# A two-layer gated mixer block on one core: low weight parts by adding DMAs, and a start with unsplit modulation products and six early chunks

## The chip, the core and the metric

The kernel runs on one core of a Trainium2 chip. The core has a matrix engine (PE, with its weight loads shown apart as PEld), three elementwise engines (DVE, ACT, POOL), a queue engine (SP) that issues DMAs, and 16 DMA engines. The metric is the device time of one execution in microseconds. Of three runs of the kernel before, the median is 1831.37 us (1830.43 to 1831.96).

## The reference, cut to what matters

Two layers (DEPTH = 2) work on a sequence `x` of 512 tokens and a context of 256 tokens, both 1024 wide. In each layer a modulation is computed from one vector per stream, the normalized input is scaled and shifted by it, and one wide projection feeds four branches (retention, short convolution, long convolution, attention), which are gated, merged and projected back:

```python
m = silu(c) @ w_mod + b_mod                    # shift, scale, gate: 3 x 1024, for c and for c_ctx
h = rmsnorm(x, norm_w) * (1 + scale) + shift
p = h @ w_in                                   # 6912 columns for the branches, 4 x 1024 for the gates
merged = sum(sigmoid(g_i) * (branch_i @ w_branch[i]) for i in range(4))
x = x + gate * (merged @ w_out)
```

In the second layer the context needs only its keys, values and retention states. All is float32.

## The kernel before, in words

Features lie on the 128 partitions and tokens along the free dimension, so a chunk of 128 output features is a chain of products over eight 128x128 blocks of the weights, accumulated in one PSUM bank. To get float32 accuracy out of the fast `float32r` form, both operands are split into a high part (a rounded copy) and a low part (the value minus its high part); a block then takes three products, high by high, high by low and low by high (`mm3`, L478). A chunk has 24 products: 256 columns each for a context stream, 512 for an `x` stream. There are four streams in a row, named by layer: c0 (context), x0, c1 (context, keys and values only), x1.

Weights are loaded by SP in the order of use (`w_load`, L425): for a context stream as two halves of 128x512 in arena rows, for an `x` stream as one 128x1024 tile in one of two `wraw` buffers. `w_split` (L445) makes the parts in one of three `wt` buffers: ACT copies the high part, DVE subtracts it from the raw tile for the low part. `w_ahead` (L461) keeps two chunks split ahead of the one in use. A gate chunk (kind "g") brings along a 128x512 tile of `w_branch`, split in the same way into arena rows.

The order on PE is written by the program: `Tally` (L191) counts an estimated clock, and `slot` (L337) lets generators of side work (attention, retention, convolutions) put in their products when the estimate says that their inputs are ready and that DVE and ACT aren't too far behind. The other engines' instructions are ordered by the framework, and each engine takes its own in order.

`start` (L1346) is the first stage. The modulation of layer 0 is needed in eight parts b = 0 to 7 before the context's normalized input exists. For each part four tiles of 128x512 of `w_m` are loaded (`mod_load`, L542); `mod_pe` (L559) splits each on ACT and DVE and multiplies with the vectors' four columns (high and low of both streams, `s4`), 16 products of 256 columns into four PSUM partitions; `mod_pe_end` (L572) copies the result to SBUF and turns it onto the partitions with two small products against `sel`. `modulate` (L659) then makes block b of the input, high and low. Beside this the first three projection chunks (ak, av, ax) are multiplied block by block, three iterations behind the modulation (LAG = 3).

Of the kernel before, what the change touches and what calls it, by code (L numbers as in the profile page):

```python
# [22 lines left out]
LAG = 3  # L23
PINS = 3

P = 128
# [164 lines left out]
class Tally:  # L191
# [14 lines left out]
    def add(self, eng, op, a, k):  # L206
# [4 lines left out]
        if eng == "tensor":  # L211
            if op == "transpose":
                d = 0.109
            elif aps[2].dtype == F32:
                d = max(0.218, aps[2].free_size() / 600)
            else:
                d = aps[2].free_size() / 2400
                if aps[2].dtype == F32R and d < 0.1:
                    d = 0.213
            self.now += d  # L220
            end = self.now + 0.15
        else:
# [12 lines left out]
            end = start + d + 0.15  # L235
            if eng == "sync":
                end += 2.0 + n * out.shape[0] / 90000
# [40 lines left out]
class Block:  # L278
    def __init__(self, ctx, tc, xc, vec, cst, w_a, w_g, w_b, w_o, w_m, out, out2):
# [5 lines left out]
        rp = ctx.enter_context(tc.tile_pool(name="rp", bufs=1))  # L285
        rp.tile([P, PAD], F32, name="fill")
        self.arena = Arena(rp, NROWS, 12)
# [9 lines left out]
        self.vec = cp.tile([P, NV], F32, name="vec")  # L297
        nc.sync.dma_start(self.vec, vec)
# [6 lines left out]
        self.turn = {}  # L305
        self.wq, self.wraws, self.wready, self.wkeep = [], [], {}, {}
        self.lanes = [[] for _ in range(5)]
        self.turns = 0
# [73 lines left out]
    def get_banks(self, n):  # L382

        while True:
            i = self.turn.get("work", 0)
            ready = max(self.nc.over(self.work[(i + j) % 4]) for j in range(n))
# [38 lines left out]
    def w_load(self):  # L425
# [4 lines left out]
        if small:  # L430
            raws = [(self.row(), slice(o, o + 512)) for o in (0, 512)]
            for r, o in raws:
                nc.sync.dma_start(r.a, src[:, o])
            raws = [(r, r.a, o) for r, o in raws]
        else:
            raw = self.take("wraw")
            nc.sync.dma_start(raw, src)
            raws = [(None, raw, slice(0, 1024))]
        if kind == "g":
            r = self.row()  # L440
            nc.sync.dma_start(r.a, self.wsrc["b"][l, i])
            raws.append((r, r.a, None))
        self.wraws.append((key, raws))

    def w_split(self):  # L445
        nc = self.nc
        key, raws = self.wraws.pop(0)
        parts = [self.take("wt")]
        for _, raw, o in raws:
            if o is None:  # L450
# [77 lines left out]
    def csilu(self):  # L528
# [8 lines left out]
        nc.vector.tensor_scalar(self.cs.rearrange("p a b -> p (a b)"), t2, 0.5, None, op0=ALU.mult)  # L537
        self.s4 = self.cp.tile([P, KC, 4], F32R, name="s4")
        nc.scalar.activation(self.s4[:, :, 0:2], self.cs, AF.Copy)
        nc.vector.tensor_tensor(self.s4[:, :, 2:4], self.cs, self.s4[:, :, 0:2].bitcast(F32), op=ALU.subtract)  # L540

# [16 lines left out]

    def mod_pe(self, tiles):  # L559
        nc = self.nc  # L560
        ps = self.bank_now()
        for h, t in enumerate(tiles):
            hi, lo = self.part(), self.part()
            nc.scalar.activation(hi.r, t.a, AF.Copy)
            nc.vector.tensor_tensor(lo.r, t.a, hi.a, op=ALU.subtract)
            for i, x in enumerate((hi, lo)):
                for k in range(2):
                    nc.tensor.matmul(ps[0:4, 0:256], self.s4[:, 2 * h + k], x.r[:, k * 256:k * 256 + 256],
                                     start=(h == 0 and i == 0 and k == 0), stop=(h == 3 and i == 1 and k == 1))
        return ps  # L570

    def mod_pe_end(self, l, b, ps):  # L572
        m4 = self.small("m4", [4, 256], 4)
        self.nc.scalar.activation(m4, ps[0:4, 0:256], AF.Copy)
        for j in range(2):
            self.nc.tensor.matmul(ps[:, 256 + 2 * j:258 + 2 * j], m4[:, cs(j)], self.c("sel")[0:4],
                                  start=True, stop=True)
        self.mod_add(l, b, ps[:, 256:], 2)
# [759 lines left out]

    def load_row(self, st, k):

        o, w = (0, SEQ) if st.s == 0 else (SEQ, CTX)
        x = self.row(w)
        self.nc.sync.dma_start(x.a, self.xd[st.s][k] if st.l else self.xc[k, :, o:o + w])
        return x

    def start(self, st):  # L1346

        nc = self.nc
        loads = [self.mod_load(0, 0)]
        st.x = self.load_x(st)  # L1350
        self.csilu()
        acc = None
        for k in range(KC):
            acc = self.square(st.x[k].a, acc)
        names = [("ak", 0), ("av", 0), ("ax", 0)]
        self.early = {}
        ws, pss = [], []
        mods = {}

        def dense(k):  # L1360
            for w, ps in zip(ws, pss):
                self.mm3(ps, w, [None] * k + [st.hx[k]] + [None] * (KC - 1 - k), ks=[k])

        for k in range(KC + LAG):
            if k + 1 < KC:
                loads.append(self.mod_load(0, k + 1))
            if k < 3:
                ws.append(self.w_get("a", st, CIDX[names[k]], False)[0])
                pss.append(self.take("dense")[:, :st.t])
                self.early[st, CIDX[names[k]]] = pss[-1]  # L1370
            if k < KC:
                mods[k] = self.mod_pe(loads.pop(0))
            if 1 <= k <= KC:
                self.mod_pe_end(0, k - 1, mods.pop(k - 1))
            if k == 1:
                res = []
                for _ in self.rms(acc, res):
                    pass
# [6 lines left out]
        st.x = st.rstd = None  # L1385

# [123 lines left out]
```

## Time and profile before

| what | value |
|---|---|
| median of three runs | 1831.37 us |
| profiled execution, its own time | 1828.66 us |
| its span from first to last instruction | 1826.9 us |
| mean granted clock of PE | 0.997 |
| matrix products | 10242 |
| DMA traffic | 232.60 MB, mean 127 GB/s |

The span is the time between the first and the last instruction of the profiled execution; its own time has 1.8 us around it. The trace gives for each instruction its engine, its start and its length, what ended the idle time before it, and for each DMA the time from issue to landing. Products overlap in their pipeline, so the time that one more product costs is the distance between starts, not its length. Nearly all instructions stand under line 187, the helper that records them, so groups go by tile names: `w`, `wh` and `wl` are a raw weight tile and its parts, `r` an arena row, `d` a PSUM bank of the chunks, `k` a working bank, `s` the modulation's vectors, `s_m` the copied modulation, `cst` constants.

### The profile page before, as it was taken

What the parts mean: (1) busy time and instruction counts of PE and PEld (TensorE: products, weight loads), DVE (VectorE), ACT (ScalarE), POOL (GpSimd) and SP (SyncE); (2) the same over time, 40 slices, a digit from 0 to 9 for tenths busy, and PEclk for the clock granted to TensorE, in tenths of its full rate; (3) what the DMA queues carried; (4) which work ended last, traced back from release to release, by engine and by line L of the source; (5) the groups of instructions that cost most, each with busy time, mean ns of one, the idle gap of its engine ahead of it and who ended that gap; (6) DMA issues with size and microseconds to landing.
All of it is one profiled execution on the core that took longest, in us unless ns stands there. A gap on an engine that the chain in (4) does not pass through costs nothing. (4 is left out here: it accounts for less than half of the span.)

```text
span 1826.9 us, 27582 instructions
## 1 busy us (share of the span) xinstructions
PE 1798.4 (98%) x10242; PEld 1562.3 (86%) x10242; DVE 1326.9 (73%) x2635; ACT 851.6 (47%) x1625; POOL 27.9 (2%) x34
## 2 busy tenths in 40 slices
PE   6999999999999999999999999999999999999998
PEld 4999999988888888888888889888888888888888
DVE  8899999884556669996998457447999866344445
ACT  6666765553554544423423246445534554323223
POOL 1000000000000000000000000000000000000000
PEclk9999999999999999999999999999999999999999
DMA  9646477743222222233555552322222232332233
GB/s 315 246 129 207 120 239 231 233 138 116 70 70 68 83 81 80 95 113 124 183 167 170 159 190 76 116 70 70 65 92 84 84 95 91 111 105 90 87 116 116
DMA packets 104135, 232.60 MB, mean 127 GB/s; under 512 B 12864, under 2 KB 19776, under 8 KB 104000
## 3 DMA queue, kind: packets, MB, share of 16 engines
q1 hardware_dynamic: 104000, 230.84, 39.1%
q8 instruction: 80, 1.31, 0.3%
q14 instruction: 55, 0.45, 0.1%
HBM read 218.73 MB, written 5.24 MB: 123 GB/s over the span
## 5 line engine op out<-in xcount | busy, mean ns | idle before, releaser
L187 PE MATMUL d<-r,wh 128*128 128x512 f32 (+1 forms) x3136 | 942.8, 383 | 0.3 <-DVE r L187 0.3
L187 PEld LDWEIGHTS d<-r,wh 128*128 128x128 f32 x3136 | 572.7, 188 | 106.2 <-DVE r L187 0.8
L187 PE MATMUL d<-r,wl 128*128 128x512 f32 (+1 forms) x1568 | 597.6, 381 | 0.0
L187 DVE TENSOR_TENSOR wl<-w,wh 128x1024 fp32r<-128x1024 f32 x193 | 235.8, 1222 | 234.7 <-ACT wh L187 228.8
L187 ACT ACTIVATE wh<-w 128x1024 fp32r<-128x1024 f32 x193 | 204.9, 1062 | 412.0 <-PE d L187 354.8
L187 PEld LDWEIGHTS d<-r,wl 128*128 128x128 f32 x1568 | 294.8, 188 | 57.8
L187 ACT ACTIVATE r<-r 128x512 fp32r<-128x512 f32 (+3 forms) x264 | 150.6, 588 | 206.6 <-DVE r L187 93.8
L187 DVE TENSOR_TENSOR r<-r,r 128x512 fp32r<-128x512 f32 (+5 forms) x337 | 207.6, 630 | 33.4 <-ACT r L187 29.5
L187 DVE SCALAR_TENSOR_TENSOR r<-r,h_cfw,r 128x503 f32<-128x503 f32 (+19 forms) x360 | 229.4, 649 | 2.0
L187 PE MATMUL d<-r,r 128*128 128x512 f32 x768 | 184.8, 389 | 0.5 <-DVE r L187 0.5
L187 ACT ACTIVATE wh<-r 128x512 fp32r<-128x512 f32 x208 | 129.2, 630 | 101.7 <-PE d L187 90.0
L187 PEld LDWEIGHTS d<-r,r 128*128 128x128 f32 x768 | 144.1, 188 | 30.8 <-DVE r L187 0.9
L187 DVE TENSOR_TENSOR wl<-r,wh 128x512 fp32r<-128x512 f32 x208 | 140.6, 685 | 18.6 <-ACT wh L187 17.6
L187 DVE SCALAR_TENSOR_TENSOR r<-r,d 128x512 f32<-128x512 f32 (+1 forms) x156 | 92.8, 595 | 55.1 <-PE d L187 32.4
L187 ACT ACTIVATE r<-d 128x512 f32<-128x512 f32 (+2 forms) x234 | 118.5, 507 | 14.1 <-PE d L187 9.5
L187 PE MATMUL k<-r,r 128*128 128x128 f32 (+2 forms) x752 | 112.3, 290 | 2.7 <-ACT p L187 2.6
L187 ACT ACTIVATE r<-k 128x512 fp32r<-128x512 f32 (+4 forms) x162 | 77.0, 523 | 70.2 <-PE k L187 68.7
L187 PEld LDWEIGHTS k<-r,r 128*128 128x128 f32 x752 | 99.5, 191 | 9.0 <-ACT p L187 6.2
L187 ACT ACTIVATE p<-k,s_nm 128x256 f32<-128x256 f32 (+1 forms) x144 | 69.7, 496 | 77.0 <-DVE s_nm L187 76.8
L187 DVE SCALAR_TENSOR_TENSOR r<-r,cs,r 128x256 f32<-128x256 f32 x196 | 83.8, 480 | 1.0 <-DMA r<-w_m 0.4
L187 DVE TENSOR_TENSOR r<-k,r 128x512 fp32r<-128x512 f32 (+2 forms) x88 | 54.5, 653 | 9.2 <-ACT r L187 9.0
L187 ACT ACTIVATE p<-p,s_rc 128x512 f32<-128x512 f32 (+2 forms) x80 | 51.3, 719 | 8.6 <-DVE s_rc L187 8.6
(400 smaller groups left out, 2249.0 us busy)
## 6 DMA issues: line engine op xcount, KB each, us to landing
w<-w_a SPq DMA_DIRECT2D x108, 512.0 KB, 3.5
r<-w_a SPq DMA_DIRECT2D x128, 256.0 KB, 4.8
w<-w_g SPq DMA_DIRECT2D x64, 512.0 KB, 3.5
r<-w_m SPq DMA_DIRECT2D x96, 256.0 KB, 3.8
r<-w_b SPq DMA_DIRECT2D x96, 256.0 KB, 3.3
r<-w_g SPq DMA_DIRECT2D x64, 256.0 KB, 3.7
w<-w_o SPq DMA_DIRECT2D x21, 512.0 KB, 3.5
r<-xc SPq DMA_DIRECT2D x24, 256.0 KB, 3.9
```

The costliest lines, as they stand in the source:

```text
L187: return f(*a, **k)
```

## The change

The low part of a weight is no longer a subtraction on DVE in most chunks. ACT writes the negated high part into the low tile, and a DMA issued from POOL's queue then adds the weights from memory to it (`accum_op=ALU.add`). This holds for every chunk of an `x` stream and for every second chunk of a context stream (the first, third, ... that `w_split` makes); the `w_branch` tiles stay on DVE. There is a fourth `wt` buffer, and three chunks are split ahead instead of two. The vectors `vec` move into the place of the padding tile `fill`.

In `start` the modulation's products take the raw tiles unsplit, as plain float32, with a stationary operand of 32 columns (two of them used, the rest zero): eight products of 256 columns, four each into partitions 0, 32, 64 and 96 of one bank, and the selection sums the four groups. `w_m` is loaded two parts ahead instead of one. Six chunks (ak, av, ax, ay of head group 0, ax, ay of group 1) instead of three are multiplied beside it, in the three `d` banks, the `ov` bank and two working banks; their weights are split on ACT and DVE into arena rows. Products of zeros (`warm`) are put between the others, 46 of up to 512 columns in all. The context's input rows are kept in half-size rows.

```diff
@@ class Tally, add
+            elif eng == "gpsimd" and op == "dma_start":
+                d = 1.0
...
@@ class Block, __init__
-        self.wt = [[cp.tile([P, 1024], F32R, name=f"w{p}{i}") for p in "hl"] for i in range(3)]
+        self.wt = [[cp.tile([P, 1024], F32R, name=f"w{p}{i}") for p in "hl"] for i in range(4)]
@@ w_split
             nc.scalar.activation(hi, raw, AF.Copy)
-            nc.vector.tensor_tensor(lo, raw, hi.bitcast(F32), op=ALU.subtract)
+            if o and (not key[3] or self.nsplit % 2):
+                nc.scalar.activation(lo, hi.bitcast(F32), AF.Copy, scale=-1.0)
+                nc.gpsimd.dma_start(lo, src, accum_op=ALU.add)
+            else:
+                nc.vector.tensor_tensor(lo, raw, hi.bitcast(F32), op=ALU.subtract)
...
-    def w_ahead(self, n=2):
+    def w_ahead(self, n=3):
@@ csilu
-        self.s4 = self.cp.tile([P, KC, 4], F32R, name="s4")
...
+        self.c32 = self.cp.tile([P, KC, 32], F32, name="c32")
+        nc.gpsimd.memset(self.c32, 0.0)
+        nc.vector.tensor_scalar(self.c32[:, :, 0:2], t2.rearrange("p (a b) -> p a b", b=2), 0.5, None, op0=ALU.mult)
@@ mod_pe
+    def mod_pe(self, tiles, warm=None):
         ps = self.bank_now()
-        for h, t in enumerate(tiles):
-            hi, lo = self.part(), self.part()
-            nc.scalar.activation(hi.r, t.a, AF.Copy)
-            nc.vector.tensor_tensor(lo.r, t.a, hi.a, op=ALU.subtract)
-            for i, x in enumerate((hi, lo)):
-                for k in range(2):
-                    nc.tensor.matmul(ps[0:4, 0:256], self.s4[:, 2 * h + k], x.r[:, k * 256:k * 256 + 256],
-                                     start=(h == 0 and i == 0 and k == 0), stop=(h == 3 and i == 1 and k == 1))
+        for k in range(KC):
+            j = 32 * (k % 4)
+            if warm and k == 4:
+                self.warm(*warm)
+            self.nc.tensor.matmul(ps[j:j + 32, 0:256], self.c32[:, k], tiles[k // 2].a[:, k % 2 * 256:k % 2 * 256 + 256],
+                                  start=k < 4, stop=k >= 4)
@@ start
+        banks = [b[:, :st.t] for b in self.dense + self.ovs + work[:2]]
...
         for k in range(KC + LAG):
+            dense(min(KC, max(0, k - LAG + 1)))
-            if k + 1 < KC:
-                loads.append(self.mod_load(0, k + 1))
-            if k < 3:
-                ws.append(self.w_get("a", st, CIDX[names[k]], False)[0])
...
+            if k + 2 < KC:
+                loads.append(self.mod_load(0, k + 2))
+            if k < len(names):
+                ws.append(self.early_weights())
             if k < KC:
-                mods[k] = self.mod_pe(loads.pop(0))
+                self.warm((14, 4, 4, 2)[k] if k < 4 else 0, idle)
+                mods[k] = self.mod_pe(loads.pop(0), (10, idle) if k == 0 else None)
...
             if 1 <= k <= KC:
                 self.modulate(st, k - 1)
-            if k >= LAG:
-                dense(k - LAG)
+            if k == len(names) - 1:
+                self.w_ahead()
```

Here `early_weights` loads the next chunk in two halves, copies the high part on ACT and subtracts on DVE, and `dense(blocks)` brings every loaded chunk up to that many blocks, three products each.

## Rows read from the trace of the kernel before

**Rows 1.** The page: busy time, share of the span, instructions of each engine.

```profile
PE 1798.4 (98%) x10242; PEld 1562.3 (86%) x10242; DVE 1326.9 (73%) x2635; ACT 851.6 (47%) x1625; POOL 27.9 (2%) x34
```

**Rows 2.** Busy time by stretch: length, five engines, granted clock, DMA share, GB/s.

```profile
0.00:53.00 53.00, 37.48 (x239) 25.20 (x240) 44.70 (x152) 34.91 (x74) 4.91 (x7) 0.94 0.93 327
53.00:200.00 147.00, 147.00 (x1229) 146.60 (x1230) 139.35 (x355) 92.02 (x215) 4.08 (x4) 1.00 0.54 176
200.00:360.00 160.00, 160.00 (x1335) 159.65 (x1334) 145.70 (x331) 97.67 (x208) 2.29 (x3) 1.00 0.69 220
450.00:800.00 350.00, 348.14 (x1785) 292.14 (x1784) 257.44 (x498) 167.59 (x338) 4.03 (x4) 1.00 0.25 82
1800.00:1827.00 27.00, 19.41 (x162) 19.04 (x160) 14.65 (x28) 9.31 (x18) 0.70 (x1) 0.94 0.38 134
```

**Rows 3.** PE's waits in 53 to 1800 us: total, times, longest.

```profile
PE k L187 <- ACT p L187: 3.4, 9, 0.7
```

**Rows 4.** PE in order of time: start, length, tiles, shape, count, idle before.

```profile
43.74 2.06 PE L187 MATMUL k<-r,s 128*4 128x256 f32 x16
45.74 0.60 PE L187 MATMUL k<-cst,s_m 4*128 4x2 f32 x4
...
52.88 0.39 PE L187 MATMUL d<-r51h,wh 128*128 128x256 f32 x1 [0.16 <-ACT r L187]
...
53.35 0.28 PE L187 MATMUL d<-r67h,wh 128*128 128x256 f32 x1
...
65.34 0.28 PE L187 MATMUL d<-r81l,wh 128*128 128x256 f32 x1
```

**Rows 5.** DVE's groups in 0 to 53 us: busy, mean ns, idle before.

```profile
L187 DVE TENSOR_TENSOR r<-r,r 128x512 fp32r<-128x512 f32 x32 | 21.3, 686 | 1.3 <-ACT r L187 1.3
L187 DVE TENSOR_TENSOR wl<-r,wh 128x512 fp32r<-128x512 f32 x8 | 5.3, 688 | 0.0
L187 DVE SCALAR_TENSOR_TENSOR r<-r,mod,r 128x256 f32<-128x256 f32 x8 | 3.8, 480 | 0.0
```

**Rows 6.** ACT in order of time: the third tile of part 1 is waited for.

```profile
14.76 1.24 ACT L187 ACTIVATE r<-r 128x512 fp32r<-128x512 f32 x2 [0.87 <-DMA r<-w_m]
```

**Rows 7.** DMA packets, bytes and mean rate in 15 to 25 us.

```profile
DMA packets 2197, 4.01 MB, mean 401 GB/s; under 512 B 242, under 2 KB 242, under 8 KB 2196
```

**Rows 8.** PE in order of time around a plain float32 product, recorded as two instructions.

```profile
417.11 0.59 PE L187 MATMUL k<-r,cst 128*128 128x256 f32 x2
417.35 0.82 PE L187 MATMUL d<-r,wh 128*128 128x512 f32 x2
418.01 0.40 PE L187 MATMUL d<-r,wl 128*128 128x512 f32 x1
418.25 0.62 PE L187 MATMUL d<-r,wh 128*128 128x512 f32 x2
418.70 0.40 PE L187 MATMUL d<-r,wl 128*128 128x512 f32 x1
```

**Rows 9.** The page's groups that make the parts of weights: busy, mean ns, idle before.

```profile
L187 DVE TENSOR_TENSOR wl<-w,wh 128x1024 fp32r<-128x1024 f32 x193 | 235.8, 1222 | 234.7 <-ACT wh L187 228.8
L187 ACT ACTIVATE wh<-w 128x1024 fp32r<-128x1024 f32 x193 | 204.9, 1062 | 412.0 <-PE d L187 354.8
L187 ACT ACTIVATE wh<-r 128x512 fp32r<-128x512 f32 x208 | 129.2, 630 | 101.7 <-PE d L187 90.0
L187 DVE TENSOR_TENSOR wl<-r,wh 128x512 fp32r<-128x512 f32 x208 | 140.6, 685 | 18.6 <-ACT wh L187 17.6
```

**Rows 10.** DMA issues in 60 to 200 us: tile, count, size, median us to landing.

```profile
r<-w_a SPq DMA_DIRECT2D x75, 256.0 KB, 4.3
```

**Rows 11.** DMA issues in 450 to 800 us.

```profile
w<-w_a SPq DMA_DIRECT2D x40, 512.0 KB, 3.4
```

**Rows 12.** POOL's groups over the span: busy, mean ns, idle before.

```profile
L187 POOL TENSOR_TENSOR s_rsr<-s_ve,cst 128x4 f32<-128x4 f32 x8 | 8.1, 1008 | 497.7 <-DVE s_ve L187 497.7
```

**Rows 13.** A DVE group over the span, from SBUF to SBUF with a scalar.

```profile
L187 DVE TENSOR_SCALAR r<-r,cs 128x256 f32<-128x256 f32 x28 | 9.1, 348 | 0.4 <-PE d L187 0.4
```

More of the change, by code (lines that the diff above doesn't have):

```diff
@@ L385, in get_banks @@
             i = self.turn.get("work", 0)
-            ready = max(self.nc.over(self.work[(i + j) % 4]) for j in range(n))
+            ready = max(self.nc.over(self.work[(i + j) % len(self.work)]) for j in range(n))
             if ready <= self.nc.now or self.flow is None:
@@ L433, in w_load @@
                 nc.sync.dma_start(r.a, src[:, o])
-            raws = [(r, r.a, o) for r, o in raws]
+            raws = [(r, r.a, o, src[:, o]) for r, o in raws]
         else:
@@ L448, in w_split @@
         parts = [self.take("wt")]
-        for _, raw, o in raws:
+        self.nsplit += 1
+        for _, raw, o, src in raws:
             if o is None:
@@ L1337, in load_x, with load_row, early_weights @@
         return [self.load_row(st, k) for k in range(KC)]
-    def load_row(self, st, k):
+    def load_row(self, st, k, keep=False):
         o, w = (0, SEQ) if st.s == 0 else (SEQ, CTX)
-        x = self.row(w)
+        x = self.row(w, keep)
         self.nc.sync.dma_start(x.a, self.xd[st.s][k] if st.l else self.xc[k, :, o:o + w])
         return x
+    def early_weights(self):
+        nc = self.nc
+        kind, l, i, _ = self.wq.pop(0)
+        ws = []
+        for o in (0, 512):
+            raw = self.row()
+            nc.sync.dma_start(raw.a, self.wsrc[kind][l, i][:, o:o + 512])
+            hi, lo = self.part(), self.part()
+            nc.scalar.activation(hi.r, raw.a, AF.Copy)
+            nc.vector.tensor_tensor(lo.r, raw.a, hi.a, op=ALU.subtract)
+            ws += [(hi, lo, cs(k)) for k in range(4)]
+        return ws
     def start(self, st):
         nc = self.nc
+        names = [("ak", 0), ("av", 0), ("ax", 0), ("ay", 0), ("ax", 1), ("ay", 1)]
+        work = self.work
+        zeros = self.row()
+        nc.gpsimd.memset(zeros.a, 0.0)
+        self.zero = zeros.a.bitcast(BF16)[:, :512]
+        idle = self.ovs[0]
+        banks = [b[:, :st.t] for b in self.dense + self.ovs + work[:2]]
+        self.work = work[2:]
         loads = [self.mod_load(0, 0)]
-        st.x = self.load_x(st)
+        st.x = [self.load_row(st, k, True) for k in range(KC)]
         self.csilu()
@@ L1354, in start, with dense @@
             acc = self.square(st.x[k].a, acc)
[L1355 to L1362, printed above, removed]
-        for k in range(KC + LAG):
-            if k + 1 < KC:
-                loads.append(self.mod_load(0, k + 1))
-            if k < 3:
-                ws.append(self.w_get("a", st, CIDX[names[k]], False)[0])
-                pss.append(self.take("dense")[:, :st.t])
-                self.early[st, CIDX[names[k]]] = pss[-1]
+        loads.append(self.mod_load(0, 1))
+        self.early = {(st, CIDX[x]): b for x, b in zip(names, banks)}
+        ws, done, mods = [], [0] * len(names), {}
+        def dense(blocks):
+            for j, w in enumerate(ws):
+                for k in range(done[j], blocks):
+                    hi, lo, c = w[k]
+                    xh, xl = st.hx[k]
+                    for n, (a, b) in enumerate(((hi, xh), (hi, xl), (lo, xh))):
+                        nc.tensor.matmul(banks[j], a.r[:, c], b.r, start=(k == 0 and n == 0),
+                                         stop=(k == KC - 1 and n == 2))
+                done[j] = max(done[j], blocks)
+        for k in range(KC + LAG):
+            dense(min(KC, max(0, k - LAG + 1)))
[3 more added lines that the diff above has]
+                ws.append(self.early_weights())
             if k < KC:
-                mods[k] = self.mod_pe(loads.pop(0))
+                self.warm((14, 4, 4, 2)[k] if k < 4 else 0, idle)
+                mods[k] = self.mod_pe(loads.pop(0), (10, idle) if k == 0 else None)
             if 1 <= k <= KC:
@@ L1375, in start @@
             if k == 1:
-                res = []
+                res, two = [], self.work
+                self.work = work[:2]
+                self.warm(4, idle)
                 for _ in self.rms(acc, res):
-                    pass
+                    self.warm(4, idle)
+                self.work = two
                 st.rstd = res[0]
```

28 lines of the change are left out of this document (14 added, 14 removed).

## The prediction, made before the changed kernel ran

> **What bounds the kernel now.** I read the busy shares first, then the stretches, then PE's waits, and only then the start in order of time. PE is busy 98% of the span, DVE 73%, ACT 47%, POOL 2% [rows 1]. The stretches show where the missing 2% lies: in the first 53 us PE is idle for 53 - 37.5 = 15.5 us, in the last 27 us for 7.6 us, and in 1747 us between for the rest of 1826.9 - 1798.4 = 28.5, that is 5.4 us [rows 1, 2]. The longest group of waits in between comes to 3.4 us over nine waits [rows 3]. So from 53 us on the time is the sum of PE's products, and whatever DVE is spared there can give back at most those 5.4 us; DVE's 139 of 147 us in the stretch that follows the start [rows 2] looks like a bound but is none, since PE is busy in all 147. What can be won lies in the start: the fourth chunk's first product begins at 52.9 us [rows 4], with three chunks done.
>
> The start is bound by DVE: 44.7 of 53 us busy, of it 21.3 us for the low parts of 32 modulation tiles [rows 2, 5]. One part of the modulation needs four of these (4 x 0.69 = 2.7 us) and two passes of 0.48 us for the input block, besides 1.4 us for a chunk's two halves while chunks come [rows 5], against 2.06 + 0.6 us on PE [rows 4]. The DMA engines are close behind, 93% at 327 GB/s [rows 2], and where nothing holds the queue back they bring 401 GB/s [rows 7].
>
> **The start, part by part.** Removed: 32 copies on ACT, 32 subtractions on DVE (21.3 us) and 128 products. Added: three more chunks to load (6 x 256 KB), 6 x 2 copies and subtractions for all six, 64 plain float32 products, 46 products of zeros. Without the 21.3 us DVE has room, so the loads are next. SP's order up to part 1 is as before, and its third tile landed at about 14.8 us [rows 6]. Behind it stand parts 2 to 7 (24 tiles) and six chunks (12 halves): 36 x 262,144 B = 9.44 MB, at 401 GB/s 23.5 us, so the last half of the sixth chunk lands at 38.3 us. Its high part (0.63) and low part (0.69) [rows 5, 9] make it 39.6 us. No row buffer holds this up: of 59 rows about 45 are held when the last part is asked for.
>
> PE takes its products in the written order, and behind the sixth chunk's arrival there still stand: 12 products that bring that chunk to block 3, four rounds of 18 for blocks 4 to 7, two parts of the modulation and three selections. A product of 256 columns costs 0.12 us: (65.34 - 53.35) / 100 products [rows 4]. 84 x 0.12 = 10.1 us. A selection is 0.6 us [rows 4], three are 1.8.
>
> No row shows a product in one of four column groups, so I bound it by the plain float32 product of 256 columns in rows 8: the first half takes 417.35 - 417.11 = 0.24 us, the second what 417.35 to 418.01 has over 418.25 to 418.70, 0.66 - 0.45 = 0.21 us, together 0.45. Eight one after the other are 3.6 us a part; if four run at once, two rounds are 0.9 us. I take 0.9, because the four write different partitions and none waits for another, and keep 3.6 as a rival. The Trainium skill, "TensorE: Matmul & The Clock Gate", Part 3 (Packing small matmuls), says that outputs at partitions 32j run concurrently and gives 2.38x for three such tiles; by that a part would be 8 x 0.45 / 3.2 = 1.1 us (an estimate from that page), and no run here shows it yet.
>
> So PE ends its six chunks at 39.6 + 10.1 + 1.8 + 2 x 0.9 = 53.3 us, if the last block comes in time. It doesn't quite: after the last selection come a copy on ACT, small DVE operations, and two passes on DVE with one on ACT between; I take 3.4 us (two of 0.48 on DVE [rows 5], the others of like size), against 18 products = 2.2 us beside it. That is 1.2 us more: 54.5 us. But 72 of these products (8.6 us) stood behind the start before, so the comparable point is 45.9 us against 52.9: 7.0 us less. The granted clock of the start was 0.94 on average [rows 2], so about 6.4 of the 53 us at the 1.2 GHz level, after PE had waited. In the changed start PE waits from about 18 us until the third chunk's arrival at 27.9 us (18 x 262,144 B at 401 GB/s behind 14.8, and the split), so the level can fall again; before 38 us waiting hides it, behind it it costs up to 3.2 us. I take 1.0. The products of zeros before 14.8 us stand beside the loads and cost nothing; if the vectors' stationary operand came late, PE would have 23 us to make it up.
>
> **After the start.** 193 low parts of 1.22 us go from DVE to ACT (about 1.06 us each) and to a DMA, and of the context's halves about every second one (0.69 to 0.63 us) [rows 9]. On ACT that makes in c0's 53 to 200 us 92 + 24 x 2 x 0.63 = 122 of 147 us, in x0's 450 to 800 us 168 + 48 x 1.06 = 219 of 350 [rows 2, 9]. ACT stays below PE, so I cost it at nothing; the cover is that a chunk is asked for when its buffer falls free, which ACT already waits for (354.8 us [rows 9]), and three chunks ahead. The chain for an x chunk is 1.06 + 1.06 on ACT, an issue on POOL, and a landing. No row shows such an issue or such a landing. For the issue the nearest is one small POOL operation, 1.0 us [rows 12], with nothing and 2 us as ends; for the landing a plain 512 KB load, 3.4 us [rows 11], with twice that as the other end, since the add must read the tile as well as write it. That is 6.5 us, at the far end 10.9, against three chunks of 24 products at 0.225 (two in 418.70 - 418.25 [rows 8]), 16 us. Covered at both ends. POOL's powers for the norms now queue behind DMAs that wait for ACT, a few us on chains that PE's order plans with slack. DMA share in x0 is 0.25 [rows 2] and at most triples.
>
> In c0 the cover is thin. Chunk time is 24 x 0.12 = 2.9 us, so three ahead are 8.6 us. The chain is 4 x 0.63 on ACT, 1.0 on POOL and 4.3 for a plain 256 KB landing [rows 10]: 7.8 us, under 8.6; with twice the landing 12.1, over it. A gate chunk has 36 products, three ahead are 13 us, over both. I take 7.8 and so no cost, since the plain landing is the one row of like size and its 4.3 us already has a loaded queue in it.
>
> Sum: -7.0 + 1.0 = -6.0 us on the profiled execution's own 1828.7 us, 1822.7. That execution is 2.7 us under the median of the runs, so the forecast for the median is 1825.4 us.
>
> **Rivals.** (1) *The adding DMAs come too late in c0* (slower). Every second chunk uses the same two of four buffers, so four chunks take the chain plus 2.9 us where that is over 11.5. It decides from a chain of 8.6 us, a landing of 5.1. With a landing between the ends (6.4 us) the chain is 9.9 us, 1.3 us over, and c0's 48 remaining projection chunks are 12 groups of four: +16 us, 1841. At the far end it is 12 x 3.5 = 42 us. For it: c0 already has a DMA share of 0.54 to 0.69 [rows 2] and ACT would be at 83%. Against it: side work stretches c0's chunk times, and each chunk's wait is PE's alone. The Trainium skill, "SBUF — State Buffer", box on the "DVE blocks DMA" trap, says that a DMA issued from GpSimd can't get its descriptors written while DVE runs a two-port operation. Here the trace has such candidates of 0.35 us [rows 13], too short and few to lift the chain by 0.8 us on most chunks; no run here shows the lock.
>
> (2) *The column groups don't overlap* (slower). A part takes 3.6 us, an iteration more than its loads, and PE is behind from the third chunk on: 27.9 + 5 x (3.6 + 0.6) + 90 x 0.12 + 0.6 + 54 x 0.12 = 66.8 us, less 8.6: 58.2, 5.3 us later than before, with the clock 6.3: 1838. The Trainium skill speaks against it, in the part of "TensorE: Matmul & The Clock Gate" named above.
>
> (3) *The loads don't reach 401 GB/s.* At the old mean of 327 [rows 2] the 9.44 MB take 28.9 us, 5.4 more, and the gain is 0.6: 1831, no change. For it: the queue was held for stretches even though DMA share was 0.93.
>
> (4) *DVE's relief is worth something.* PE's 5.4 us of waits go, at best: 1820.
>
> **How the numbers follow.** Forecast 0.50 (its own range 1821 to 1829), rival 1 0.17, rival 2 0.08, rival 3 0.15, rival 4 0.10. A measurement of this kernel tells about 0.2% (3.7 us) from no change. Faster by that: nine tenths of the forecast and rival 4, 0.55. Within: the rest of the forecast and rival 3, 0.20. Slower: rivals 1 and 2, 0.25. The range 1817 to 1843 leaves out the far half of rival 1 and a better start with all waits gone.
>
> **What would show it.** Right: the low parts of modulation tiles gone from DVE, 401 GB/s from 15 to 38 us, sixth chunk's halves landed near 38 us, the first mixer chunk's product near 54.5 us, PE still without gaps in 53 to 360 us, landings of adding DMAs under 5 us. Wrong: starts of the eight products 0.45 us apart (rival 2), PE waiting for a DMA into `wl` in c0 (rival 1), six chunks done later than 60 us, or waits of PE for ACT in x0 and x1 above the 3.4 us of before.

## The result, and the profile after

The changed kernel takes 1891.7 us (median of 4 runs, 1888.9 to 1892.7) against 1831.1 for the kernel before in the same job: ratio 1.033 (95% interval 1.031 to 1.035). The forecast was 1825.4, its range 1817 to 1843. Below, the profiled execution of the changed kernel has a span of 1890.7 us.

The page's busy times and its two large queues (answering [rows 1]; q0 is GpSimd's, q1 SyncE's: packets, MB, share of 16 engines' span):

```profile
PE 1827.3 (97%) x10286; PEld 1575.6 (83%) x10288; DVE 1036.3 (55%) x2312; ACT 1061.2 (56%) x1883; POOL 280.4 (15%) x327
...
q0 software_dynamic: 41904, 126.90, 39.7%
q1 hardware_dynamic: 104000, 230.84, 36.6%
```

DVE has fallen from 73% to 55% as the change means it to, and PE waits more. The adding DMAs move 126.9 MB for 39.7% of the engines, the loads 230.8 MB for 36.6%: per MB 0.397 x 1890.7 x 16 / 126.9 = 94.6 us of one engine against 48.0, twice as much. By stretch (columns as in [rows 2]):

```profile
0.00:53.00 53.00, 44.23 (x269) 25.70 (x272) 28.37 (x127) 19.53 (x42) 6.63 (x11) 0.84 0.86 297
53.00:200.00 147.00, 139.29 (x1143) 136.35 (x1143) 115.87 (x309) 106.34 (x238) 39.18 (x45) 0.99 0.93 244
200.00:360.00 160.00, 150.67 (x1201) 149.29 (x1200) 105.97 (x249) 105.23 (x228) 30.68 (x37) 0.96 0.89 245
450.00:800.00 350.00, 340.74 (x1740) 286.10 (x1740) 190.79 (x429) 211.30 (x385) 45.49 (x52) 0.98 0.67 151
```

In 53 to 200 us the DMA share went from 0.54 to 0.93, in 200 to 360 from 0.69 to 0.89, and PE, which had no gap there before, stands for 7.7 and 9.3 us and has part of the rest at the 1.2 GHz level (0.99, 0.96). The landings of 60 to 200 us tell why (answering [rows 10]; the last number is the median in us):

```profile
q1 hardware_dynamic: 13931, 23.71, 50.7%
q0 software_dynamic: 5468, 9.96, 41.0%
...
r<-w_a SPq DMA_DIRECT2D x80, 256.0 KB, 6.9
wl<-w_a POOLq DMA_DIRECT2D x39, 256.0 KB, 7.1
```

An adding DMA lands after 7.1 us, and the plain loads of raw weights beside it now take 6.9 in place of 4.3. What waits for these, in 53 to 450 us: PE (total, times, longest; in [rows 3] the longest group was 3.4 us over the whole stretch to 1800)

```profile
PE d L187 <- ACT r L187: 6.8, 4, 2.8
PE d L187 <- DMA wl<-w_a: 5.1, 4, 3.1
PE d L187 <- ACT wl L187: 3.4, 1, 3.4
PE k L187 <- ACT r L187: 2.8, 1, 2.8
```

and ACT:

```profile
ACT r L187 <- DMA r<-w_b: 28.5, 8, 10.0
ACT r L187 <- DMA r<-r: 14.7, 5, 7.1
```

Only 5.1 us are PE's waits for a low part that came late. The larger part goes through ACT, which takes its instructions in order: here (ACT in order of time) it stands 10 us for a late tile of `w_b`, while the evictions and halves that PE needs are queued behind it (PE's one wait for `ACT wl`, 3.4 us, follows). SP asked for that tile at 201.7 us, and it landed 7.8 us later; the median for `w_b` in c0 was 3.8 before.

```profile
198.92 0.63 ACT L187 ACTIVATE wh<-r 128x512 fp32r<-128x512 f32 x1
209.52 0.63 ACT L187 ACTIVATE r<-r 128x512 fp32r<-128x512 f32 x1 [9.96 <-DMA r<-w_b]
```

The same holds for others of PE's waits for ACT: these two lines of ACT stand ahead of waits of 1.8 and 2.8 us.

```profile
94.83 0.42 ACT L187 ACTIVATE r<-r 128x256 fp32r<-128x256 f32 x1 [7.15 <-DMA r<-r]
...
284.41 0.63 ACT L187 ACTIVATE r<-r 128x512 fp32r<-128x512 f32 x1 [6.18 <-DMA r<-w_b]
```

All of PE's waits in 53 to 450 us come to 22.5 us. The time at the 1.2 GHz level takes about 8 more, an estimate from the two clocks above: (1 - 0.99) x 147 + (1 - 0.96) x 160 = 7.9. Together that is nearly the 32 us lost between the first two marks of the next table.

Where the 61 us lie is read by counting: the products into the dense banks are the same behind the start, so the n-th from the end is the same work in every kernel. Its start in the profile, less that of before, in us:

```
n-th product from the end   8079   5479   4079    479      1
stretch that ends there    start     c0  attention x1 but   tail
                                           of x0  its tail
before, at                  77.1  447.7  848.1  1747.5  1817.7
changed kernel              +1.8  +34.1  +48.3   +57.6   +63.7
e1  start only              -1.6   -1.6   +5.6    +9.5    +9.5
e2  adds only              +14.1  +37.0  +48.5   +54.9   +60.3
e3  its order, DVE          -1.1  +11.5  +29.4   +47.2   +47.2
e4  its order, DVE negates  +0.1  +37.6  +51.2   +72.1   +78.2
e5  its order, no DMA       +0.4  +12.2  +31.1   +49.2   +49.9
e9  adds in context        +14.6  +42.0  +47.5   +59.9   +59.9
e9  adds in x               +2.3   +8.1  +22.2   +29.9   +48.8
e11 plain writes            +1.7   +8.9  +20.8   +21.3   +21.3
e13 small adds              +1.7   +3.3  +14.1   +12.2   +12.2
e8  reordered start         -0.7   -0.1   +4.2    +8.2    +8.4
e14 and zero products       -4.4   -4.2   +2.9    +6.9    +7.1
```

(The mark of c0 lies 56 us behind c0's last product, in x0's first chunks. At that last product itself the changed kernel has lost 31.1 us, the run with adds in x 2.3. The tail is the last 479 products. In e2 and the run with adds in the context, chunks of the mixer with their adds stand in the start already. The profile of before is of an execution 2.7 us under its median, so the last column is up to 3 us over what the medians say, in e13 5 and in the run with adds in x 6.)

### The profile page after: what moved, and what is told of

It is laid out like the page before. It is cut to its first block, busy times and chain, and to the rows that moved or that the text cites. A ratio compares the mean times of both kernels' runs of the same rounds, so it can differ in the third digit from the quotient of the medians.

```text
span 1890.7 us, 28115 instructions
## 1 busy us (share of the span) xinstructions
PE 1827.3 (97%) x10286; PEld 1575.6 (83%) x10288; DVE 1036.3 (55%) x2312; ACT 1061.2 (56%) x1883; POOL 280.4 (15%) x327
## 3 DMA queue, kind: packets, MB, share of 16 engines
q0 software_dynamic: 41904, 126.90, 39.7%
q1 hardware_dynamic: 104000, 230.84, 36.6%
## 4 chain that ended last, share of the span: by engine, by line
PE 77%; DMA 7%; issue 6%; DVE 5%; ACT 3%; POOL 1%; SPq 0%; POOLq 0%; DVEq 0%; ACTq 0%
PE d L187 66%; PE k L187 9%; DVE r L187 4%; PE ov L187 2%; DMA w<-w_a 2%; ACT p L187 1%; DMA wl<-w_a 1%; ACT r L187 1%; ACT wh L187 1%; DMA wl<-w_o 1%; DMA r<-w_b 1%; DMA r<-r 1%; POOL wl L187 1%; DMA r<-xc 1%; DMA r<-w_m 1%
## 5 line engine op out<-in xcount | busy, mean ns | idle before, releaser
L187 ACT ACTIVATE r<-r 128x512 fp32r<-128x512 f32 (+3 forms) x244 | 139.4, 587 | 314.1 <-DMA r<-w_b 158.2
L187 DVE TENSOR_TENSOR r<-r,r 128x512 fp32r<-128x512 f32 (+5 forms) x317 | 194.6, 628 | 157.6 <-ACT r L187 152.9
L187 ACT ACTIVATE wl<-wh 128x1024 fp32r<-128x1024 f32 (+1 forms) x291 | 264.8, 911 | 2.4
L187 POOL DMA_DIRECT2D wl<-w_a x166 | 144.6, 871 | 802.9 <-ACT wl L187 634.4
L187 DVE SCALAR_TENSOR_TENSOR r<-r,h_cfw,r 128x503 f32<-128x503 f32 (+23 forms) x360 | 225.5, 652 | 3.3
L187 POOL DMA_DIRECT2D wl<-w_g x96 | 83.0, 874 | 567.8 <-ACT wl L187 349.4
L187 ACT ACTIVATE wh<-r 128x512 fp32r<-128x512 f32 x196 | 120.6, 626 | 41.8 <-PE d L187 38.3
L187 ACT ACTIVATE r<-k 128x512 fp32r<-128x512 f32 (+5 forms) x164 | 77.4, 519 | 27.8 <-PE k L187 25.9
L187 DVE TENSOR_TENSOR wl<-r,wh 128x512 fp32r<-128x512 f32 x98 | 66.8, 688 | 39.8 <-ACT wh L187 37.5
```

What stands on the lines that cost most here:

```text
L187: return f(*a, **k)
```

## The experiments

**First four: which part.** The theories: A, the adding DMAs load the DMA engines and come late; B, the negated copies crowd ACT; C, the planner, told that DVE is nearly free, writes an order in which PE's side work comes too early. Each ran beside the kernel before, as did all others.

*Start alone* (also 63 rows, three pairs of buffers, two chunks ahead):

```
-            if o and (not key[3] or self.nsplit % 2):
+            if False:
```

> The changed start alone: low parts by DVE everywhere, three buffers and two chunks ahead as before (63 rows instead of 59, which the start needs with DVE's load counted). Theory A (the adding DMAs load the DMA engines and come late) and theory B (the negated copies crowd ACT) both expect only what the start costs, about +2 us on before: 1831 to 1836. Theory C (PE's written order, made with DVE counted as free, puts side work in too early) expects the same. If the six early chunks push work into DVE's full stretch, above 1840.

1837.9, ratio 1.0043 (1.0028 to 1.0058). The start gains 1.6 us, nothing is lost in c0, and 11 us behind it: 7 in the attention of x0, 4 up to the tail of x1. So the start isn't where 61 us went.

*Adds alone*: start and modulation of before, the rest as changed (the reverse of the diff's edits to `start`, `mod_pe` and `csilu`).

> The start of before with the adding DMAs, the fourth buffer and three chunks ahead. A, B and C all expect the loss of the changed kernel less about 2 us for the start: 1884 to 1892. Below 1870 the two parts of the change would hurt each other.

1888.7 (1.032). As expected: the adds and the order written for them make nearly all of it.

*The changed kernel's order on PE, low parts by DVE*: the planner is still told of the copy and the DMA, but what is issued is a subtraction.

```
-                nc.scalar.activation(lo, hi.bitcast(F32), AF.Copy, scale=-1.0)
-                nc.gpsimd.dma_start(lo, src, accum_op=ALU.add)
...
+                eng.vector.tensor_tensor(lo, raw, hi.bitcast(F32), op=ALU.subtract)
```

> The changed kernel with PE's order kept exactly as it is (the planner still counts the copy and the DMA), but the low parts made by DVE's subtraction. A and B expect the loss behind the start to go: 1833 to 1842. C expects it to stay: above 1875, with waits of PE for DVE in place of those for ACT.

1876.1 (1.025), where theories A and B put 1833 to 1842: an order written for a free DVE costs 46 us when DVE isn't free. It can't tell how much that order costs where DVE *is* free; e13 below does.

*Adds kept, negated copies on DVE*, PE's order as in the changed kernel:

```
-                nc.scalar.activation(lo, hi.bitcast(F32), AF.Copy, scale=-1.0)
...
+                eng.vector.tensor_scalar(lo, hi.bitcast(F32), -1.0, None, op0=ALU.mult)
```

> The changed kernel with PE's order kept, the adding DMAs kept, but the negated copy made by DVE instead of ACT. A expects most of the loss to stay: 1875 to 1895. B expects ACT, 265 us lighter, to give it back: 1833 to 1850. In between, both carry part.

1909.0 (1.043), 17 us more than the changed kernel: the lighter ACT that B puts its hope in gave nothing back. But DVE took the copies on in an order that counts it as free, so this alone doesn't rule B out. The counterpart keeps the copies on ACT and lets DVE make the sum, with no DMA for it:

```
-                nc.gpsimd.dma_start(lo, src, accum_op=ALU.add)
...
+                eng.vector.tensor_tensor(lo, raw, lo.bitcast(F32), op=ALU.add)
```

> The changed kernel's order on TensorE, and the negated copies on ScalarE as in it, but the sum by VectorE from the raw rows in the chip, with no DMA for it. Against the run in the same order with VectorE's subtraction and no negated copy (1876) it adds 256 or so ScalarE copies of 0.6 to 1.1 us; against the changed kernel it has VectorE's work back and the adding DMAs gone. If ScalarE's copies cost: more than 5 us over 1876, so 1881 to 1900. If they lie beside other work: 1872 to 1880. The loss in the context's mixer, 31.9 us with the adding DMAs, should then be near the 12.3 us of the run with subtractions, at most 18.

1877.7 (1.026), 1.6 over the run with subtractions, whose ratio is 1.025: the negated copies cost nothing that shows beside the noise, and B falls.

**Load by itself, twice missed.** The kernel before, with adding DMAs beside it whose sums nothing reads.

```
...
+            if o and (not key[3] or self.nsplit % 2):
+                self.tc.nc.gpsimd.dma_start(self.take("scr")[:, o], self.wsrc[kind][l, i][:, o], accum_op=ALU.add)
```

> The kernel before with its order, its start and its subtractions kept; beside them the same adding DMAs as in the changed kernel (every low part of x, every second one of the context), but into two tiles that nothing reads. The work they add on the DMA engines is the same, nothing waits for their data, ScalarE has no negated copies. Theory A1 (the load itself: an adding DMA takes about twice the engine time of a plain one, so the loads of raw weights, which ScalarE and TensorE stand for, come late): the mixer of the context loses 15 to 30 us, ScalarE's waits for late b rows reappear, 1850 to 1880. Theory A2 (what costs is that the products wait for the added tiles): 1830 to 1836.

2313 (1.265), far outside both. With two tiles, an add stands in GpSimd's own queue until an earlier add into its tile has landed, and GpSimd (POOL) also makes the norms' powers; DVE's wait for one of them is on the page (busy, mean | idle before, ended by):

```profile
L187 DVE TENSOR_SCALAR r<-r,s_mv,s_rsr 128x128 f32<-128x128 f32 x40 | 12.2, 344 | 217.6 <-POOL s_rsr L187 217.6
```

So the run measured a blocked queue, not the load. With four half tiles, in the context alone:

> The load alone again, mended: the kernel before, and beside it the adding DMAs of the context's every second low part into four half tiles in turn, so that GpSimd's queue doesn't stand for a tile that is still being written (with two it did, and GpSimd's statistics came late: 2313). No result is read, nothing else is changed. If load in the DMA engines alone delays what the mixer stands for: 20 to 40 us lost in the context's mixer, 1850 to 1872. If the cost of the adds is in the waits for their own data and in ScalarE's negated copies: 1830 to 1836.

1933.9 (1.056), a miss again: an add that waits for no copy isn't paced, so GpSimd issued them from the first microseconds on, as fast as four tiles let it. While they ran, the DMA engines were full and PE had 32.5 of 70 us:

```profile
130.00:200.00 70.00, 32.53 (x257) 32.16 (x255) 23.51 (x52) 17.86 (x42) 30.36 (x37) 0.76 1.11 256
200.00:300.00 100.00, 92.10 (x736) 91.10 (x737) 95.10 (x263) 54.91 (x130) 14.69 (x16) 0.95 0.63 177
```

102 us are lost by the time the adds end, and none after. But not all of it is load: DVE stood once more for a GpSimd operation behind the adds (176 to 202 us), and PE behind DVE. The second line is ACT's in 30 to 300 us, the third PE's.

```profile
DVE s_tab_sx L187 <- POOL s_tab_u L187: 25.6, 1, 25.6
```

```profile
ACT r L187 <- DMA r<-r: 48.5, 8, 23.1
```

```profile
PE d L187 <- DVE wl L187: 23.4, 2, 22.8
```

So 22.8 us of PE's are the blocked queue again. Two other stands of PE, 17.7 and 17.8 us, follow ACT's waits for late loads: that load can stop PE is shown, but its price in the changed kernel isn't.

**What of an add costs.** One word out, all engines' lists and waits the same (low parts hold the weights):

```
-                nc.gpsimd.dma_start(lo, src, accum_op=ALU.add)
+                nc.gpsimd.dma_start(lo, src)
```

> The changed kernel with one word out: the DMAs of the low parts write their bytes in place of adding them (so the low parts hold the weights themselves and the output is another). Every engine's list of instructions is the changed kernel's, every wait stays, the same bytes come from memory; only the read of the target and the sum are gone. If the doubled engine time of an adding DMA (327 against 159 ns a packet of 4 KB) is what delays the loads, the DMA share in the context's mixer falls from 0.93 to about 0.75, ScalarE's waits for late rows there from 40 us to under 15, and the time comes to 1845 to 1865. If a second stream of the same bytes is what costs, added or not (memory's rate, one more queue, the landing of 6 us before a use), the time stays at 1880 to 1892.

1852.0 (1.011, 1.009 to 1.013): 39.7 us of the 61 are in that word. The time is where the first answer put it, but the DMA share and ACT's waits for `w_b` (19.3 us) and `r` (5.1) fell less than it said. The same bytes by the same queue now take 0.223 x 1849.8 x 16 / 126.9 = 52.0 us of an engine per MB, not 94.6:

```profile
q1 hardware_dynamic: 104000, 230.84, 37.0%
q0 software_dynamic: 41904, 126.90, 22.3%
```

The stretch behind the start, and then the landing of a plain write in the place of an add in 60 to 200 us:

```profile
53.00:200.00 147.00, 144.71 (x1210) 142.93 (x1209) 120.51 (x320) 111.32 (x249) 26.98 (x47) 1.00 0.81 265
```

```profile
wl<-w_a POOLq DMA_DIRECT2D x40, 256.0 KB, 5.4
```

The loss to the end of c0 falls from 34 us to 9, and those in x1 and in the tail vanish. The run doesn't tell the adds' load from their lateness: a plain write's own chain, 4 x 0.63 + 0.54 for the issue + 5.4 = 8.5 us, is just under the cover of 8.6. PE's and ACT's waits in the changed kernel speak for the load. Next the bytes themselves, with each add cut to 64 columns (the planner is told of the whole one, and the rest of a low part keeps the negated copy):

```
-                nc.gpsimd.dma_start(lo, src, accum_op=ALU.add)
...
+                self.tc.nc.gpsimd.dma_start(lo[:, :64], src[:, :64], accum_op=ALU.add)
```

> The changed kernel with the adding DMAs cut to 64 of the 512 (or 1024) columns of each low part, so the rest of a low part holds the negated copy and the output is another. Every engine's instructions, their order and their waits are the changed kernel's; the second stream of bytes is nearly gone (its bytes fall to about an eleventh). What is left over 1830 is then the planned order, the negated copies and the start. If the second stream of bytes is the whole of what the run with plain writes still lost (21 us): 1830 to 1836. If the written order and ScalarE's copies hold it: 1846 to 1854, with the loss of 10 us in the context's mixer and 12 in the attention of x where that run had them.

1837.7 (1.0034, 1.0022 to 1.0047): between the two answers. Another 14.3 us go with the plain second stream, its bytes and its landings (3.9 us for 5.4). ACT's waits for `w_b` in 53 to 450 us fall along: 28.5, 19.3 and now 11.1 us, against 3.4 before. The 7.4 left are order, start and copies; the profile (of an execution 3.4 us above the median) has +10.8 in the attention of x0.

**Where the adds cost.** Start of before, 63 rows, three pairs, two ahead; once only the context's adds, once only x's:

```
+            if o and key[3] and self.nsplit % 2:
```

> The start of before; adding DMAs only for every second low part of the context's weights, all others by VectorE's subtraction; three pairs of weight buffers, two chunks made ahead. If the context's mixer is lost to the load of the adding DMAs beside its own loads (all adds: 36 us at its end), this run loses 20 to 36 us there and then no more than the 8 us that every new plan loses in x: 1850 to 1875. If the loss comes from the adds in x, which stand in the same queues, 1830 to 1842.

```
+            if o and not key[3]:
```

> The counterpart: adding DMAs only for x's weights (half of the loads in time: 16 us a chunk of 1 MB), VectorE's subtraction for the context; three pairs of buffers, two chunks ahead. If the load beside crowded loads is what costs, the context's mixer is that of before within 3 us and x loses 8 to 20 us: 1838 to 1852. If adds cost wherever they stand (a late tile stops the products), x alone loses 25 us or more: over 1855.

1891.6 (1.034) and 1872.7 (1.024), the first above both of its answers, the second in the range of adds that cost wherever they stand. The context's adds cost 42 us to the mark of c0 and 18 behind it, where only c1's adds stand; that the order is to blame for these is not shown. Those of x cost 2 us by c0's last product, as expected there, then 6 in x0's first 56 us, 22 up to the tail and 19 in it (in an execution 5 us above its median). With two chunks ahead PE waits for x's low parts themselves:

```profile
PE d L187 <- DMA wl<-w_a: 14.2, 5, 4.1
PE d L187 <- DMA wl<-w_o: 11.3, 6, 2.9
```

**The start.** In the changed kernel (ACT in order of time) ACT is a ring of waits, 5.7 us a turn:

```profile
41.30 0.51 ACT L187 ACTIVATE r84h<-r,mod 128x256 fp32r<-128x256 f32 x1 [1.28 <-DVE r L187]
41.72 1.14 ACT L187 ACTIVATE r<-r 128x512 fp32r<-128x512 f32 x2
45.26 0.38 ACT L187 ACTIVATE s_m<-k 128x256 f32<-128x256 f32 x1 [2.41 <-PE k L187]
47.00 0.51 ACT L187 ACTIVATE r96h<-r,mod 128x256 fp32r<-128x256 f32 x1 [1.35 <-DVE r L187]
47.41 1.13 ACT L187 ACTIVATE r<-r 128x512 fp32r<-128x512 f32 x2
```

`s_m<-k` waits for the next modulation products on PE; these stand behind the new chunk's products, these behind its halves, and the halves (`r<-r`, no wait for a DMA) behind `modulate` and the `s_m` before. The edit puts the chunk's products last:

```
-            dense(min(KC, max(0, k - LAG + 1)))
             if k + 2 < KC:
...
                 self.modulate(st, k - 1)
+            dense(min(KC, max(0, k - LAG + 1)))
```

> The changed start with VectorE's low parts and no adding DMA, as in the run of the start alone (1837.9), with one edit: in the loop over the early chunks the products of a new chunk stand behind the next column-group products and their end, not ahead of them. If a ring through ScalarE's order held the start (copies of a chunk wait behind a modulation that waits for products queued behind the chunk's own), the iteration falls from 5.7 us towards 4, the first product of the mixer comes 5 to 8 us earlier than the 63 us of the changed kernel, and the time falls to 1828 to 1833. If the start is held by the loads or by the sum of ScalarE's own work, the first mixer product stays within 2 us of 63 and the time at 1836 to 1840.

1837.4 (1.0041), against 1837.9 without the edit: the second answer, so moving the ring gave nothing by itself. The third selection is 7 us earlier (24.8 for 32.0), but the first mixer product is at 61.0 us for 60.0. PE stood 0.9 and 0.7 us for the second and third chunk, and from 28.2 to 41.8 us the granted clock was at the 1.2 GHz level. Busy times and mean granted clock in 24 to 44 us:

```profile
24.00:44.00 20.00, 16.38 (x103) 11.32 (x96) 10.75 (x31) 7.23 (x15) 0.00 (x0) 0.66 0.95 365
```

So, 16 zero products into a bank not yet used, ahead of three early chunks:

```
...
+                if not done[j] and blocks and 1 <= j <= 3:
+                    for _ in range((4, 8, 4)[j - 1]):
+                        self.tc.nc.tensor.matmul(work[1], self.zero[:, :P], self.zero, start=True, stop=True)
```

> The start with the reordered loop, and besides 16 zero products (4, 8 and 4) ahead of the second, third and fourth early chunk, where TensorE stood idle and its granted clock then fell to the 1.2 GHz level for 13.7 us (28.2 to 41.8). If that level is what kept the reordered start from gaining, the period of the middle iterations falls from 6.3 us to 4, the first mixer product comes at 55 to 57 us in place of 61.0, and the time is 4 to 6 us under that run's 1837.4: 1831.5 to 1833.5. If the loads of the modulation's weights hold the iterations, the first mixer product stays at 60 to 62 and the time at 1836 to 1839.

1835.5 (1.0029, 1.0018 to 1.004), the first mixer product at 57.2 us:

```profile
24.00:44.00 20.00, 17.79 (x147) 11.81 (x148) 13.84 (x36) 10.13 (x21) 0.00 (x0) 1.00 0.98 374
```

In this stretch the clock stays at 2.4 GHz, and the start stands 4.4 us under that of before in place of 1.8 over it, most of the forecast's 6.0. The total gained less than expected (1.9 us), as x still loses 11.

**The attention of x.** Five runs on that loss. A control first, the kernel before with 63 rows:

```
-NROWS = 59
+NROWS = 63
```

> A control: the kernel before with 63 rows of the arena in place of 59 (the number that the run of the start alone needed), and nothing else. If a planned order that is merely another one costs by itself what the start alone lost in the attention of x (9 us), this one loses some of it too: 1834 to 1842. If that loss belongs to the new start, the time stays within 3 us of 1830.

1832.0 (1.0009, 0.9999 to 1.0018), but its order on PE is nearly that of before, so it shows that rows cost nothing and little on orders. Then, on e14, one chunk of x made ahead in place of two, which was to take the copy that stands for a pair of buffers from ahead of an exponential:

```
-        while len(self.wready) < n and self.wraws:
+        while self.wraws and len(self.wready) < (n if self.wraws[0][0][3] else 1):
```

> The start with zero products and VectorE's low parts, and one edit: in x the parts of one chunk are made ahead in place of two; TensorE's order stays (a shift of 0.3 products in the mean). In the run without the edit the first attention of x lost 9.4 us; ScalarE's exponentials stood there behind a copy of a weight chunk that waited for a pair of buffers which TensorE's last product had to free (698.2 us). If that place in ScalarE's order is the cause, the copy finds its pair free, the waits for the exponentials fall from 10.7 to about 4 us, and the time comes to 1824 to 1829, under both kernels. If the order of TensorE itself leaves the softmax no cover, it stays at 1833 to 1837; if the parts now come too late for the products, 1840 to 1860.

1834.7 (1.003); the waits for exponentials stay at 10.7 us. But at the longest of them, below, the copy still stands ahead of the exponential, so the run doesn't rule ACT's order out. With four pairs and 59 rows besides:

> As the run with one chunk made ahead in x, but with four pairs of buffers and 59 rows in place of three and 63: a copy never waits for a pair. If a pair still being read is what holds ScalarE's copies, this is at or under the other by 0 to 3 us: 1822 to 1829; if not, it is equal to it.

1833.9 (1.002, 1.0011 to 1.0029), and the copy stands there still. With a dearer ACT in the planner:

```
-                d = 0.1 + n / 1200
+                d = 0.15 + n / 1000
```

> The start with zero products and two chunks ahead, and the planner told a dearer ScalarE (0.15 us and 1 ns an element in place of 0.1 and 0.83; 512 elements measure 0.57), so that it orders the attention of x anew. If the loss in the attention of x is one of the planned order, it moves by several us to either side: 1826 to 1840; the waits for the exponentials (10.7 us) move with it. If it is not, it stays at 1835.5.

1834.0 (1.0022, 1.0013 to 1.003), x0 losing 3.5 us in place of 7.1: a new order moves that loss, but the total not beyond the noise. And the control on the kernel before:

> A control: the kernel before with one chunk of x's weights made ahead in place of two, nothing else. It waits 3.4 us for exponentials in all, so at most 2 us are to be had: 1827 to 1831 if the copies' place is what costs, 1830 to 1840 if the parts come late.

1832.4 (1.0014, 1.0005 to 1.0023): there the edit wins nothing. What the trace of the run with one ahead shows, DVE and then ACT in order of time, at a wait of PE of 3.1 us:

```profile
697.12 0.74 DVE L187 SCALAR_TENSOR_TENSOR r<-r,h_cfw,r 128x508 f32<-128x508 f32 x1
697.77 0.15 DVE L187 TENSOR_TENSOR s_mc<-s_mc,s_mx 128x2 f32<-128x2 f32 x1
697.84 0.73 DVE L187 SCALAR_TENSOR_TENSOR r<-r,h_cfw,r 128x499 f32<-128x499 f32 x1
698.49 0.15 DVE L187 SCALAR_TENSOR_TENSOR s_nm<-s_mc,h_nsink 128x2 f32<-128x2 f32 x1
```

```profile
698.16 1.06 ACT L187 ACTIVATE wh<-w 128x1024 fp32r<-128x1024 f32 x1 [6.16 <-issue]
699.24 0.58 ACT L187 ACTIVATE p<-k,s_nm 128x384 f32<-128x384 f32 x1
```

The row maximum that the exponential needs is ready at 698.6, made on a DVE without a gap between convolution passes (`h_cfw`) that the plan put there. The exponential starts 0.6 us later, when ACT's copy of a weight ends. So both orders, DVE's and ACT's, have a part in this wait; that they are the cause of the loss is read from it, not shown by a run. None of the versions beats the kernel before.

## Why the prediction was wrong

**The step that failed most** is the one for c0: "I take 7.8 and so no cost, since the plain landing is the one row of like size". The chain measures 4 x 0.63 + 0.87 for the issue + 7.1 = 10.5 us, between the ends given and over the 8.6 of cover. The larger omission is what the forecast's sum had no term for: the adds' time in the DMA engines that all loads share. The share of x0 was bounded ("at most triples", measured 0.67 for 0.25). That of c0, 0.54 to 0.69 before, is named in rival 1, but what the adds would bring to it was not worked out; it had no room for 41% more. c0 lost 32 us to its mark (34.1 - 1.8), of which 7 are left with plain writes (8.9 - 1.7). That the shared engines cost more of it than the adds' own lateness is read from the waits, not shown by a run of its own.

**Rival 1** had the place, the sign and the range (16 to 42 us, in c0), with a chance of 0.17; its wait was the smaller part. PE waiting for `wl` is 5.1 us; ACT's 28.5 us for `w_b` stopped PE behind it, and the clock fell with PE's gaps. By that rival's sum the measured chain would have cost 12 x (10.5 - 8.6) = 23 us in waits for `wl` alone. The two-port operations of DVE that the prediction weighed there don't explain the 40 us that e11 gave back: its plain writes go by the same queue beside the same DVE instructions.

**x was costed at nothing.** It lost 14 us in x0 and 9 up to the tail of x1, and 6 in the tail, where PE waits for low parts of `w_o`:

```profile
1844.94 0.39 PE L187 MATMUL d<-r,wl 128*128 128x256 f32 x1 [1.94 <-DMA wl<-w_o]
```

The forecast's 16 us of cover hold for products of 512 columns and a landing of 6.5 us. The tail's products have 256, so three chunks cover 8.6 us there, and the chain is 1.06 + 1.04 + 0.86 + 7.8 = 10.8, the last term being the median landing of `w_o`'s adds in 1800 to 1880 us. e11 shows the adding to be nearly all of the loss in x1 and the tail, while x0 keeps 11 to 12 us with plain writes (e11) or hardly any bytes (e13). What is left there is the planned order, which the forecast assumed to stay without gaps, and the copies, which e5 finds to cost nothing. Waits for ACT in x "above the 3.4 us of before" were named as a sign against it: those for exponentials came to 13.4 us in all.

**The start: -6.0 forecast, +1.8 measured.** The loads held: 403 and 396 GB/s, and rival 3 falls.

```profile
15.00:25.00 10.00, 9.10 (x41) 4.27 (x42) 5.85 (x38) 1.58 (x5) 0.69 (x1) 0.67 1.05 403
25.00:38.00 13.00, 10.53 (x64) 7.32 (x58) 8.95 (x27) 5.78 (x12) 0.00 (x0) 0.63 1.04 396
```

The column groups held too (rival 2 falls): a part takes 1.07 us at 2.4 GHz and 1.94 at 1.2, against 0.9 taken. The estimate by the Trainium skill, "TensorE: Matmul & The Clock Gate", Part 3, was 1.1, and the trace agrees.

```profile
24.71 1.07 PE L187 MATMUL k<-r,c 128*32 128x256 f32 x16
32.24 1.94 PE L187 MATMUL k<-r,c 128*32 128x256 f32 x16
```

What failed is "Its high part (0.63) and low part (0.69) [rows 5, 9] make it 39.6 us": SP asked for the sixth chunk at 34 us and a half took 5.1 to land, but its split begins at 47.4 us, because ACT came to it only then, and the first mixer product stands at 63.4, not 54.5. The sum followed the last transfer and let every engine be free when it came; e8 moved the ring and gave nothing, e14 shows the clock, costed at 1.0 us, to be worth 3.7 of it.

**What held.** ACT's copies cost nothing (e5 against e3). That DVE's relief is worth nothing also held: e13 relieves DVE with hardly any bytes added and is still 7.4 us slower, so rival 4 falls.

## What to carry to other kernels

Before a transfer is added, add its time in the DMA engines to the share of each stretch, for all queues together, and look for whoever stands in an in-order queue for the loads it delays; its own lateness may be the smaller cost. A busy engine that isn't the bound is no reason to move its work to a resource that others wait for. And where a planner writes the order, an edit of costs or of the start rewrites everything behind it: keep the order and change one operation (as e11 and e13 do) before a difference is put down to that operation.

## What the runs showed of the hardware

An adding DMA from memory into SBUF took 1.8 times the engine time of a plain write of the same bytes by the same queue (94.6 us per MB in the changed kernel, 52.0 in e11), and its issue on GpSimd 0.87 us against 0.54. The landing of a 256 KB add was 7.1 us against 5.4 for the plain one beside the same loads.
